# Seven half-size products for the first 512 rows of the last FFN and MLP block

## The chip, the cores and the metric

One core of one Trainium2 chip. The metric is the device time of one execution in microseconds. The kernel before was run three times: 2468.09, 2470.43 and 2472.05 us, median 2470.43 us. A further execution was profiled; its rows are read below.

## What is computed

Two stacks of two layers on 512 tokens of width 1024, all in float32. The parts that the change touches are the four feed-forward units, two of each kind:

```python
def swiglu_ffn(x, w_gate, w_up, w_down):          # first stack, layers 0 and 1, inner width 2816
    return (jax.nn.silu(x @ w_gate) * (x @ w_up)) @ w_down

x = layer_norm(ALPHA * x + y, ln_ffn_g[l], ln_ffn_b[l])

def sq_relu_mlp(h, w_up, w_down):                 # second stack, two layers, inner width 4096
    u = jax.nn.relu(h @ w_up)
    return (u * u) @ w_down
```

After FFN 0 comes a pooling mixer, after FFN 1 the first unit of the second stack, a gated linear attention (GLA). After MLP 0 comes a sliding-window attention, after MLP 1 the output norm.

## The kernel before, in words

The residual `r` stays on chip as four tiles of 128 tokens by 1024. A matrix product in float32 is made as three matmuls (`mm3`, lines 178 to 182) of a high and a low part of each operand: `split` (L151) rounds on ScalarE (L152, the high part) and subtracts on VectorE (L153, the low part). Weights are split the same way, 512 KB raw at a time; where a norm's gain goes into them, the splits are L172 and L173. There are four buffers for split weights, five for raw ones, and eight PSUM banks.

The inner width of a feed-forward unit is worked through in blocks: 1024, 1024 and 768 for an FFN, four times 1024 for an MLP. `hidden` (L941 and L1065) computes a block's activations in chunks of 512 inner rows. The product of a finished block with the down weights is added into `r` by `down_steps` (L235): instead of eight products of quarter blocks it makes seven, of sums and differences of the quarters (a Strassen-Winograd scheme). The sums are VectorE work: of the activations (`sum`), and of the weights (`chain`, from raw weights that come by DMA on SyncE's queue). Each product leaves its two PSUM banks through `resid` (L450), one addition into `r` per bank and place. `weave` (L226) alternates steps of `down_steps` with steps of `hidden` for the next block.

The last block has no next block. Its activations are split once, plainly (`hidh`, `hidl`), and `lin_out` (L361) multiplies them with the down weights in the order of line 376, tile by tile, into one bank per tile and half, followed by the residual addition. When both halves of a tile are there, `ln_tile` (L443; statistics L436 and L438, the two passes L447 and L448, the power of the variance on GpSimd in `rstd`, L423) normalizes it, and the callback of the next unit transposes it on TensorE. For GLA this is `next_unit` (L635): sum of squares on ScalarE (L615), `rstd` on GpSimd, scaling on ScalarE (L640) into `z`, then eight transposes per tile (L415) and their splits into `xTh` and `xTl`. For FFN 0 it is `next_pool` (L589), and key products from the stored memory (`kv_k`, L809, called at L1253) stand between.

The order on each engine is set by the tile framework's scheduler from priorities and its own costs; each engine then runs its list in that order, so that an instruction that waits holds up what stands behind it.

Of the kernel before, what the change touches and what calls it, by code (L numbers as in the profile page):

```python
# [11 lines left out]
F32R = mybir.dt.float32r  # L12
# [60 lines left out]
class Net:  # L73
# [151 lines left out]

    def weave(self, main, side, per):  # L226

        main, side = iter(main), iter(side)
        for _ in main:
            for _ in range(per):  # L230
                next(side, None)
        for _ in side:
            pass

    def down_steps(self, h, W, k0, first, ahead=60):  # L235
# [6 lines left out]
        nc = self.nc  # L242
        lo, hi = slice(0, 256), slice(256, 512)
        a11, a21, a12, a22 = h[0][:, :, lo], h[0][:, :, hi], h[1][:, :, lo], h[1][:, :, hi]
        sums = self.slot([128, 2, 4, 256], name="sum")
        s1, s2 = sums[:, 0], sums[:, 1]
        chain = self.slot([128, 4, 512], name="chain")
        tt = nc.vector.tensor_tensor
        done = set()

        def left(src):
            d = self.slot([128, 2, 4, 256], F32R, "A")
            self.split(d[:, 0], d[:, 1], src)
            return d

        def block(i, j):
            return [self.raw2(W, k0 + 4 * i + k, 512 * j) for k in (0, 2)]

        def plain(i, j):
            return [self.wsplit(b) for b in block(i, j)]  # L260

        def halves(t):
            return [t[:, 0:2], t[:, 2:4]]

        def product(ops, banks, start):
            d, us = ops
            for t in range(2):
                tk = slice(t * 128, t * 128 + 128)
                for k in range(4):
                    u = us[k // 2]  # L270
                    self.mm3(banks[t], d[:, 0, k, tk], d[:, 1, k, tk], u[:, 0, k % 2], u[:, 1, k % 2],
                             start and k == 0, k == 3, skip_group_check=not start)

        def out(i, j, banks, op=ALU.add):
            for t in range(2):
# [660 lines left out]
    def ffn(self, l, nxt, aside):  # L936
        nc, a = self.nc, self.a
        xT = self.pair_view(self.hi, self.lo)
        lg, lb = self.gains("ln_ffn", l)

        def hidden(b0, bw, to, split):  # L941
            for c in range(-(-bw // 512)):
                w = min(512, bw - c * 512)
                sg = self.slot([128, 4, 512], name="sg")
                to.append(sg)
                silu = lambda f, ps, t0, t1, sg=sg: nc.scalar.activation(sg[:, f, t0:t1], ps, AF.Silu)

                def ev_up(f, ps, t0, t1, sg=sg, c=c):
                    s = sg[:, f, t0:t1]
                    nc.vector.tensor_tensor(s, s, ps, ALU.mult)  # L950
                    if split:
                        self.split(split[0][c][:, f, t0:t1], split[1][c][:, f, t0:t1], s)
                if b0 == 0 and c == 0:
                    self.lin_a(xT, a["ffn_wg"][l], 0, silu, halves=True)
                else:
                    yield from self.lin_steps(xT, a["ffn_wg"][l], b0 + c * 512, silu, w)
                yield from self.lin_steps(xT, a["ffn_wu"][l], b0 + c * 512, ev_up, w)

        h = []
        for _ in hidden(0, 1024, h, None):  # L960
            pass
        for b0, bw in ((1024, 1024), (2048, 768)):
            more = []
            out = self.new_xT("hid", 2) if bw < 1024 else None
            self.weave(self.down_steps(h, a["ffn_wd"][l], (b0 - 1024) // 128, b0 == 1024),
                       hidden(b0, bw, more, out), 2)
            h = more
        self.lin_out(self.pair_view(*out), a["ffn_wd"][l], False, (lg, lb), nxt, aside=aside, k0=16, nk=6)

# [88 lines left out]
    def mlp(self, l, nxt):  # L1060
        nc, a = self.nc, self.a
# [2 lines left out]

        def hidden(b, to, split):  # L1065
            for c in range(2):
                if not split:
                    to.append(self.slot([128, 4, 512], name="h"))

                def ev_up(f, ps, t0, t1, c=c):  # L1070
                    u = self.tmp()[:, :t1 - t0]
                    nc.scalar.activation(u, ps, AF.Relu)
                    if split:
                        nc.vector.tensor_tensor(u, u, u, ALU.mult)
                        self.split(split[0][c][:, f, t0:t1], split[1][c][:, f, t0:t1], u)
                    else:
                        nc.vector.tensor_tensor(to[c][:, f, t0:t1], u, u, ALU.mult)
                if b == 0 and c == 0:
                    self.lin_a(xT, W, 0, ev_up, halves=True, gain=g)
                else:  # L1080
                    yield from self.lin_steps(xT, W, b * 1024 + c * 512, ev_up, 512, gain=g)

        h = []
        for _ in hidden(0, h, None):
            pass
        for b in range(1, 4):
            more = []
            out = self.new_xT("hid") if b == 3 else None
            self.weave(self.down_steps(h, a["w_down_2"][l], 8 * b - 8, False), hidden(b, more, out), 1)
            h = more  # L1090
        self.lin_out(self.pair_view(*out), a["w_down_2"][l], False, None, nxt, k0=24, nk=8)

    def rel_bias(self):
        nc, a = self.nc, self.a
# [204 lines left out]
```

## Time and profile before

| what | us |
|---|---|
| median of three runs | 2470.43 |
| profiled execution, device time | 2471.44 |
| its span in the profile | 2469.6 |
| TensorE matmuls busy | 2414.4 (98%) |
| VectorE busy | 1509.4 (61%) |
| ScalarE busy | 1024.4 (41%) |

The page names PE for TensorE, DVE for VectorE, ACT for ScalarE, POOL for GpSimd and SP for SyncE. Busy matmuls overlap in the pipeline, so that a full row says that PE waited for nothing, not that it ran at its peak; the spacing of the starts gives the rate. Some 1.8 us of the device time lie outside the span. The mean granted clock of the execution was 0.989.

### The profile page before, as it was taken

Reading aid. Unit: us, or ns where it says so; the run is one execution under the profiler, and the core shown is the slowest. Engines: PE = TensorE matmul, PEld = TensorE weight load, DVE = VectorE, ACT = ScalarE, POOL = GpSimd, SP = SyncE. Lnnn points to the kernel's source line nnn. Section 1 sums busy time; section 2 is a strip of 40 time slices with the busy share of each in tenths; the row PEclk is TensorE's granted clock in tenths of the full one; section 3 lists DMA queues with packets and bytes.
Section 4 is the critical chain, followed back from the end, with each engine's and each line's share of the span. In section 5 each row is a group of like instructions: output and inputs, shape, how many; then the busy total and the mean of one; then the engine's idle time right before and its main releaser. Section 6 shows DMA issues by size and latency. Waiting matters only on the chain.

```text
span 2469.6 us, 30360 instructions
## 1 busy us (share of the span) xinstructions
PE 2414.4 (98%) x12094; PEld 2010.3 (81%) x12094; DVE 1509.4 (61%) x1994; ACT 1024.4 (41%) x1620; POOL 180.5 (7%) x219
## 2 busy tenths in 40 slices
PE   8989999999999999999999999999999999999998
PEld 8877787888888997888888786888888877888887
DVE  4799475555566766455566423466876467487674
ACT  3653343233333343233334633534444456444443
POOL 1151200000000000000002003200000100000000
PEclk9999899999999999999999999999999999999999
DMA  6333122235344342334434123235553411144452
GB/s 234 103 103 111 54 83 81 84 112 171 109 143 153 126 133 77 94 132 141 141 124 132 60 86 42 87 111 171 179 172 119 161 62 52 60 171 150 155 173 77
DMA packets 148990, 291.92 MB, mean 118 GB/s; under 512 B 9449, under 2 KB 15909, under 8 KB 148592
## 3 DMA queue, kind: packets, MB, share of 16 engines
q1 hardware_dynamic: 146176, 282.17, 34.4%
q0 software_dynamic: 2096, 6.76, 1.4%
q8 instruction: 95, 1.56, 0.2%
q10 hardware_dynamic: 576, 1.05, 0.1%
q14 instruction: 47, 0.39, 0.0%
HBM read 286.77 MB, written 6.32 MB: 119 GB/s over the span
## 4 chain that ended last, share of the span: by engine, by line
PE 88%; DVE 7%; ACT 2%; issue 1%; DMA 1%; POOL 0%; SPq 0%; POOLq 0%; DVEq 0%; ACTq 0%
PE mm L180 23%; PE mm L181 23%; PE mm L182 23%; PE aux L182 5%; PE aux L180 4%; PE aux L181 4%; DVE acc L686 2%; PE aux L415 2%; PE aux L742 1%; DVE w L153 1%; PE mm L769 1%; PE mm L766 1%; PE aux L1219 0%; DVE bn L436 0%; ACT A L152 0%
## 5 line engine op out<-in xcount | busy, mean ns | idle before, releaser
L181 PE MATMUL mm<-xTl,w 128*128 128x512 f32 (+1 forms) x1696 | 614.3, 363 | 2.2 <-DVE xTl L153 2.2
L180 PE MATMUL mm<-xTh,w 128*128 128x512 f32 (+1 forms) x1696 | 611.4, 363 | 2.8 <-ACT w L172 1.8
L182 PE MATMUL mm<-xTh,w 128*128 128x512 f32 (+1 forms) x1696 | 574.0, 362 | 0.0
L153 DVE TENSOR_TENSOR w<-raw,w 128x1024 fp32r<-128x1024 f32 (+1 forms) x286 | 340.4, 1195 | 349.2 <-ACT w L152 348.9
L152 ACT ACTIVATE w<-raw 128x1024 fp32r<-128x1024 f32 (+1 forms) x286 | 293.6, 1030 | 579.4 <-PE mm L182 460.3
L180 PEld LDWEIGHTS mm<-xTh,w 128*128 128x128 f32 x1696 | 320.5, 190 | 53.2 <-ACT w L172 2.6
L181 PEld LDWEIGHTS mm<-xTl,w 128*128 128x128 f32 x1696 | 321.6, 190 | 50.9 <-DVE xTl L153 2.4
L182 PEld LDWEIGHTS mm<-xTh,w 128*128 128x128 f32 x1696 | 320.4, 190 | 48.8
L173 DVE SCALAR_TENSOR_TENSOR w<-raw,gains_T,w 128x512 fp32r<-128x512 f32 (+1 forms) x200 | 140.7, 736 | 122.1 <-ACT w L172 121.6
L172 ACT ACTIVATE w<-raw,gains_T 128x512 fp32r<-128x512 f32 (+1 forms) x200 | 131.1, 707 | 149.0 <-PE mm L182 141.6
L180 PE MATMUL aux<-w,A 128*128 128x512 f32 x440 | 169.6, 391 | 2.1 <-ACT A L152 2.1
L181 PE MATMUL aux<-w,A 128*128 128x512 f32 x440 | 171.4, 390 | 0.0
L182 PE MATMUL aux<-w,A 128*128 128x512 f32 x440 | 170.1, 391 | 1.1 <-DVE A L153 0.7
L181 PE MATMUL mm<-w,xTh 128*128 128x512 f32 (+1 forms) x352 | 135.1, 384 | 0.0
L182 PE MATMUL mm<-w,xTl 128*128 128x512 f32 (+1 forms) x352 | 134.6, 385 | 0.0
L180 PE MATMUL mm<-w,xTh 128*128 128x512 f32 (+1 forms) x352 | 134.6, 385 | 0.0
L152 ACT ACTIVATE w<-chain 128x1024 fp32r<-128x1024 f32 x60 | 63.8, 1063 | 133.4 <-DVE chain L305 52.5
L180 PEld LDWEIGHTS aux<-w,A 128*128 128x128 f32 x440 | 82.6, 188 | 22.7 <-ACT A L152 5.8
L182 PEld LDWEIGHTS aux<-w,A 128*128 128x128 f32 x440 | 82.6, 188 | 21.0 <-DVE A L153 4.1
L181 PEld LDWEIGHTS aux<-w,A 128*128 128x128 f32 x440 | 82.6, 188 | 16.9
L455 DVE TENSOR_TENSOR r<-r,mm 128x512 f32<-128x512 f32 x76 | 51.4, 682 | 55.8 <-PE mm L182 55.8
L153 DVE TENSOR_TENSOR xTl<-aux,xTh 128x512 fp32r<-128x512 f32 x72 | 47.3, 682 | 60.1 <-ACT xTh L152 60.1
(358 smaller groups left out, 4186.9 us busy)
## 6 DMA issues: line engine op xcount, KB each, us to landing
raw<-in_w_down SPq DMA_DIRECT2D x124, 512.0 KB, 3.6
raw<-in_ffn_wd SPq DMA_DIRECT2D x84, 512.0 KB, 3.4
raw<-in_w_up SPq DMA_DIRECT2D x64, 512.0 KB, 4.6
raw<-in_ffn_wg SPq DMA_DIRECT2D x40, 512.0 KB, 3.8
raw<-in_ffn_wu SPq DMA_DIRECT2D x40, 512.0 KB, 3.6
raw<-in_ab_w_in SPq DMA_DIRECT2D x24, 512.0 KB, 4.2
raw<-in_a_w_in SPq DMA_DIRECT2D x24, 512.0 KB, 3.6
raw<-in_xa_wk SPq DMA_DIRECT2D x16, 512.0 KB, 3.4
```

The costliest lines, as they stand in the source:

```text
L152: self.nc.scalar.activation(hi, src, AF.Copy)
L153: self.nc.vector.tensor_tensor(lo, src, hi.bitcast(F32), ALU.subtract)
L172: nc.scalar.activation(u[:, 0, i], raw[:, i], AF.Identity, scale=g)
L173: nc.vector.scalar_tensor_tensor(u[:, 1, i], raw[:, i], g, u[:, 0, i].bitcast(F32), ALU.mult, ALU.subtract)
L180: nc.tensor.matmul(ps, lh, rh, start=start, stop=False, **kw)
L181: nc.tensor.matmul(ps, lh, rl, start=False, stop=False, **kw)
L182: nc.tensor.matmul(ps, ll, rh, start=False, stop=stop, **kw)
L415: self.nc.tensor.transpose(ps[:, j, :], src[:, j * 128:j * 128 + 128], self.ident)
L455: self.nc.vector.tensor_tensor(r, r, ps, op)
L686: nc.vector.scalar_tensor_tensor(dst, src, col, dst, ALU.mult, ALU.add)
L742: nc.tensor.matmul(d[:, h - h0, :], ke[rows, t, h * 128:h * 128 + 128], vh(t, h)[rows, :], start=True, stop=True)
L766: nc.tensor.matmul(o, P[:, h, :], vh(t, h), start=True, stop=False)
```

## The change

`down_steps` takes the number of 128-row pieces of a quarter from the activations that it gets: four as before, or two. In each FFN and MLP, the first 512 inner rows of the last block now also go through it, as quarters of 256 inner rows by 256 tokens; their chunk of `hidden` is no longer split plainly. It runs behind the preceding block's `down_steps` as one list of steps, woven with the last block's `hidden` by a list of counts. `lin_out` keeps 256 inner rows in an FFN (before 768) and 512 in an MLP (before 1024).

```diff
--- before.py
+++ after.py
@@ -225,9 +225,9 @@
 
     def weave(self, main, side, per):
 
-        main, side = iter(main), iter(side)
-        for _ in main:
-            for _ in range(per):
+        side = iter(side)
+        for i, _ in enumerate(main):
+            for _ in range(per[min(i, len(per) - 1)]):
                 next(side, None)
         for _ in side:
             pass
@@ -242,34 +242,35 @@
         nc = self.nc
         lo, hi = slice(0, 256), slice(256, 512)
         a11, a21, a12, a22 = h[0][:, :, lo], h[0][:, :, hi], h[1][:, :, lo], h[1][:, :, hi]
-        sums = self.slot([128, 2, 4, 256], name="sum")
+        nk = h[0].shape[1]
+        sums = self.slot([128, 2, nk, 256], name="sum")
         s1, s2 = sums[:, 0], sums[:, 1]
-        chain = self.slot([128, 4, 512], name="chain")
+        chain = self.slot([128, nk, 512], name="chain")
         tt = nc.vector.tensor_tensor
         done = set()
 
         def left(src):
-            d = self.slot([128, 2, 4, 256], F32R, "A")
+            d = self.slot([128, 2, nk, 256], F32R, "A")
             self.split(d[:, 0], d[:, 1], src)
             return d
 
         def block(i, j):
-            return [self.raw2(W, k0 + 4 * i + k, 512 * j) for k in (0, 2)]
+            return [self.raw2(W, k0 + nk * i + k, 512 * j) for k in range(0, nk, 2)]
 
         def plain(i, j):
             return [self.wsplit(b) for b in block(i, j)]
 
         def halves(t):
-            return [t[:, 0:2], t[:, 2:4]]
+            return [t[:, k:k + 2] for k in range(0, nk, 2)]
 
         def product(ops, banks, start):
             d, us = ops
             for t in range(2):
                 tk = slice(t * 128, t * 128 + 128)
-                for k in range(4):
+                for k in range(nk):
                     u = us[k // 2]
                     self.mm3(banks[t], d[:, 0, k, tk], d[:, 1, k, tk], u[:, 0, k % 2], u[:, 1, k % 2],
-                             start and k == 0, k == 3, skip_group_check=not start)
+                             start and k == 0, k == nk - 1, skip_group_check=not start)
 
         def out(i, j, banks, op=ALU.add):
             for t in range(2):
@@ -941,15 +942,16 @@
         def hidden(b0, bw, to, split):
             for c in range(-(-bw // 512)):
                 w = min(512, bw - c * 512)
+                plain = split if c else None
                 sg = self.slot([128, 4, 512], name="sg")
                 to.append(sg)
                 silu = lambda f, ps, t0, t1, sg=sg: nc.scalar.activation(sg[:, f, t0:t1], ps, AF.Silu)
 
-                def ev_up(f, ps, t0, t1, sg=sg, c=c):
+                def ev_up(f, ps, t0, t1, sg=sg, plain=plain):
                     s = sg[:, f, t0:t1]
                     nc.vector.tensor_tensor(s, s, ps, ALU.mult)
-                    if split:
-                        self.split(split[0][c][:, f, t0:t1], split[1][c][:, f, t0:t1], s)
+                    if plain:
+                        self.split(plain[0][0][:, f, t0:t1], plain[1][0][:, f, t0:t1], s)
                 if b0 == 0 and c == 0:
                     self.lin_a(xT, a["ffn_wg"][l], 0, silu, halves=True)
                 else:
@@ -959,13 +961,17 @@
         h = []
         for _ in hidden(0, 1024, h, None):
             pass
-        for b0, bw in ((1024, 1024), (2048, 768)):
-            more = []
-            out = self.new_xT("hid", 2) if bw < 1024 else None
-            self.weave(self.down_steps(h, a["ffn_wd"][l], (b0 - 1024) // 128, b0 == 1024),
-                       hidden(b0, bw, more, out), 2)
-            h = more
-        self.lin_out(self.pair_view(*out), a["ffn_wd"][l], False, (lg, lb), nxt, aside=aside, k0=16, nk=6)
+        Wd = a["ffn_wd"][l]
+        more = []
+        self.weave(self.down_steps(h, Wd, 0, True), hidden(1024, 1024, more, None), [2])
+        h, last = more, []
+        out = self.new_xT("hid", 1)
+
+        def downs():
+            yield from self.down_steps(h, Wd, 8, False)
+            yield from self.down_steps([last[0][:, 0:2], last[0][:, 2:4]], Wd, 16, False)
+        self.weave(downs(), hidden(2048, 768, last, out), [2, 2, 2, 2, 1])
+        self.lin_out(self.pair_view(*out), Wd, False, (lg, lb), nxt, aside=aside, k0=20, nk=2)
 
 
 
@@ -1064,15 +1070,16 @@
 
         def hidden(b, to, split):
             for c in range(2):
-                if not split:
+                plain = split if c else None
+                if not plain:
                     to.append(self.slot([128, 4, 512], name="h"))
 
-                def ev_up(f, ps, t0, t1, c=c):
+                def ev_up(f, ps, t0, t1, c=c, plain=plain):
                     u = self.tmp()[:, :t1 - t0]
                     nc.scalar.activation(u, ps, AF.Relu)
-                    if split:
+                    if plain:
                         nc.vector.tensor_tensor(u, u, u, ALU.mult)
-                        self.split(split[0][c][:, f, t0:t1], split[1][c][:, f, t0:t1], u)
+                        self.split(plain[0][0][:, f, t0:t1], plain[1][0][:, f, t0:t1], u)
                     else:
                         nc.vector.tensor_tensor(to[c][:, f, t0:t1], u, u, ALU.mult)
                 if b == 0 and c == 0:
@@ -1083,12 +1090,19 @@
         h = []
         for _ in hidden(0, h, None):
             pass
-        for b in range(1, 4):
+        W2 = a["w_down_2"][l]
+        for b in range(1, 3):
             more = []
-            out = self.new_xT("hid") if b == 3 else None
-            self.weave(self.down_steps(h, a["w_down_2"][l], 8 * b - 8, False), hidden(b, more, out), 1)
+            self.weave(self.down_steps(h, W2, 8 * b - 8, False), hidden(b, more, None), [1])
             h = more
-        self.lin_out(self.pair_view(*out), a["w_down_2"][l], False, None, nxt, k0=24, nk=8)
+        more = []
+        out = self.new_xT("hid", 1)
+
+        def downs():
+            yield from self.down_steps(h, W2, 16, False)
+            yield from self.down_steps([more[0][:, 0:2], more[0][:, 2:4]], W2, 24, False)
+        self.weave(downs(), hidden(3, more, out), [1, 1, 1, 1, 0, 1])
+        self.lin_out(self.pair_view(*out), W2, False, None, nxt, k0=28, nk=4)
 
     def rel_bias(self):
         nc, a = self.nc, self.a
```

Where instructions stand, on TensorE at the end of FFN 1 (`mm` with `hidh` is the closing product, one bank per tile and half; `aux` with `z` are the transposes of a tile; the last `mm` rows are GLA's projections). Before:

```order
L180 MATMUL mm_10150<-wb_9936,hidh_9208 128x512 [waits DVE_49]
L181 MATMUL mm_10150<-wb_9941,hidh_9208 128x512
L415 MATMUL aux_10045<-consts,z_10039 128x128 [waits Activation_49]
L415 MATMUL aux_10052<-consts,z_10039 128x128 x4
L182 MATMUL mm_10150<-wb_9941,hidl_9210 128x512
L182 MATMUL mm_10150<-wb_9946,hidl_9211 128x512
L180 MATMUL mm_10201<-wb_9936,hidh_9208 128x512 [waits DVE_49]
L182 MATMUL mm_10201<-wb_9946,hidl_9211 128x512
L415 MATMUL aux_10096<-consts,z_10090 128x128 [waits Activation_49]
L415 MATMUL aux_10103<-consts,z_10090 128x128 [waits DVE_49]
L180 MATMUL mm_10281<-xTh_9964,wz_9954 128x256 [waits Activation_49,Pool_49]
L180 MATMUL mm_10307<-w_10255,xTh_9964 128x512
```

With the change, the same place:

```order
L180 MATMUL mm_10262<-w_10133,hidh_9256 128x512 [waits DVE_49]
L180 MATMUL mm_10270<-wb_10138,hidh_9256 128x512 [waits DVE_49]
L182 MATMUL mm_10270<-wb_10138,hidl_9257 128x512
L180 MATMUL mm_10309<-wb_10138,hidh_9256 128x512 [waits DVE_49]
L182 MATMUL mm_10309<-wb_10138,hidl_9257 128x512
L416 MATMUL aux_10201<-consts,z_10195 128x128 [waits Activation_49]
L416 MATMUL aux_10208<-consts,z_10195 128x128 x4
L416 MATMUL aux_10240<-consts,z_10234 128x128 [waits Activation_49]
L416 MATMUL aux_10247<-consts,z_10234 128x128 [waits DVE_49]
L180 MATMUL mm_10377<-xTh_10156,wz_10146 128x256 [waits Activation_49,Pool_49]
L180 MATMUL mm_10403<-w_10351,xTh_10156 128x512
```

Before, the transposes of tile 0 stand 28 matmuls ahead of the closing product's last row and those of tile 1 directly behind it; with the change the transposes of both tiles stand behind its last row, one after the other, and the projections behind both.

On VectorE at the same place (`bn` and `mv` are the statistics of a tile, `r_86` is tile 0). Before:

```order
L455 TENSOR_TENSOR r_86<-r_86,mm_10008 128x512 [waits PE_49]
L436 BN_STATS bn_10028<-r_86 128x6 [waits DVE_49]
L438 BN_AGGR mv_10031<-bn_10028 128x2 [waits DVE_49]
L447 SCALAR_TENSOR_TENSOR r_86<-r_86,mv_10031,w4k_7803 128x1024 [waits DVE_49]
L448 SCALAR_TENSOR_TENSOR r_86<-r_86,rs_10033,w4k_7805 128x1024 [waits DVE_49,Pool_49]
L455 TENSOR_TENSOR r_88<-r_88,mm_10059 128x512 [waits PE_49]
L436 BN_STATS bn_10079<-r_88 128x6 [waits DVE_49]
```

With the change:

```order
L456 TENSOR_TENSOR r_86<-r_86,mm_10160 128x512 [waits PE_49]
L456 TENSOR_TENSOR r_88<-r_88,mm_10168 128x512 [waits PE_49]
L456 TENSOR_TENSOR r_110<-r_110,aux_9864 128x512 [waits PE_49]
L437 BN_STATS bn_10184<-r_86 128x6 [waits DVE_49]
...
L456 TENSOR_TENSOR r_112<-r_112,mm_10309 128x512 [waits PE_49]
L437 BN_STATS bn_10317<-r_112 128x6 [waits DVE_49]
L439 BN_AGGR mv_10187<-bn_10184 128x2 [waits DVE_49]
L437 BN_STATS bn_10278<-r_110 128x6 [waits DVE_49]
L437 BN_STATS bn_10317<-r_112 128x6 [waits DVE_49]
L448 SCALAR_TENSOR_TENSOR r_86<-r_86,mv_10187,w4k_7851 128x1024 [waits DVE_49]
L449 SCALAR_TENSOR_TENSOR r_86<-r_86,rs_10189,w4k_7853 128x1024 [waits DVE_49,Pool_49]
```

Before, tile 0 is normalized as soon as its second half is added; now the additions and statistics of all four tiles, ten additions and eight statistics in all, stand ahead of its two passes.

On TensorE at the end of FFN 0, with the change (`mh` is the stored memory, `bands` the pooling of tile 0):

```order
L180 MATMUL mm_6118<-wb_5951,hidh_5069 128x512 [waits DVE_49]
L182 MATMUL mm_6118<-wb_5951,hidl_5070 128x512
L180 MATMUL mm_6179<-mh_5956,w_6161 128x256 [waits DVE_49,Activation_49]
L180 MATMUL mm_6303<-mh_5956,w_6285 128x256 [waits DVE_49,Activation_49]
L603 MATMUL aux_6000<-bands_5964,r_86 128x16 [waits DMASW1_49,DVE_49]
```

The key products stand between the closing product and the first instruction that needs a normalized tile, as they did before.

On VectorE in the woven last block of FFN 1, with the change (`A` are split activations, `w` from `chain` split weight differences):

```order
L153 TENSOR_TENSOR A_9932<-sum_9862,A_9932 128x512 [waits Activation_49]
L153 TENSOR_TENSOR A_9979<-sum_9862,A_9979 128x512 [waits Activation_49]
L456 TENSOR_TENSOR r_88<-r_88,mm_9916 128x512 [waits PE_49]
L153 TENSOR_TENSOR w_9940<-chain_9863,w_9940 128x1024 [waits Activation_49]
L153 TENSOR_TENSOR w_9945<-raw_9943,w_9945 128x512 [waits DMAHW1_49,Activation_49]
L315 TENSOR_TENSOR raw_10023<-raw_10023,raw_10025 128x1024 [waits DMAHW5_49,DMAHW4_49]
L306 TENSOR_TENSOR chain_9863<-raw_9982,chain_9863 128x1024 [waits DMAHW2_49,DVE_49]
L456 TENSOR_TENSOR r_110<-r_110,aux_9962 128x512 [waits PE_49]
L456 TENSOR_TENSOR r_112<-r_112,mm_9963 128x512 [waits PE_49]
L153 TENSOR_TENSOR w_9985<-chain_9863,w_9985 128x1024 [waits Activation_49]
L153 TENSOR_TENSOR w_9990<-raw_9988,w_9990 128x512 [waits DMAHW3_49,Activation_49]
```

None of these stood there before; each product of the added seven needs an `A`, two `w` and a resid of the banks before it.

## Rows read from the trace of the kernel before

**Rows 1.** Section 1 of the page: busy us, share of span, instructions.

```profile
PE 2414.4 (98%) x12094; PEld 2010.3 (81%) x12094; DVE 1509.4 (61%) x1994; ACT 1024.4 (41%) x1620; POOL 180.5 (7%) x219
```

**Rows 2.** Section 4 of the page: the chain of waits, by engine.

```profile
PE 88%; DVE 7%; ACT 2%; issue 1%; DMA 1%; POOL 0%; SPq 0%; POOLq 0%; DVEq 0%; ACTq 0%
```

**Rows 3.** PE's waits, 990:1316, then 740:870 (total us, times, longest).

```profile
PE aux L415 <- DVE r L448: 0.3, 1, 0.3
...
PE aux L415 <- DVE r L448: 0.8, 1, 0.8
```

**Rows 4.** Stretches ending FFN 1: us; PE, PEld, DVE, ACT, POOL busy; clock.

```profile
1260.00:1290.00 30.00, 30.00 (x134) 24.80 (x133) 19.84 (x24) 11.47 (x14) 0.00 (x0) 1.00 0.29 87
1290.00:1317.00 27.00, 27.00 (x121) 22.36 (x120) 12.40 (x16) 9.54 (x13) 3.47 (x4) 1.00 0.44 145
1317.00:1340.00 23.00, 23.00 (x103) 19.02 (x103) 18.18 (x26) 8.92 (x14) 6.15 (x10) 1.00 0.43 139
1340.00:1357.00 17.00, 16.66 (x83) 13.81 (x82) 16.01 (x24) 8.85 (x14) 5.05 (x8) 1.00 0.31 98
```

**Rows 5.** DVE by line, whole span: busy us, mean ns, idle before.

```profile
L455 DVE TENSOR_TENSOR r<-r,aux 128x512 f32<-128x512 f32 x96 | 65.3, 680 | 23.5 <-PE aux L182 23.4
L153 DVE TENSOR_TENSOR w<-chain,w 128x1024 fp32r<-128x1024 f32 x60 | 71.9, 1217 | 11.1 <-ACT w L152 11.1
```

**Rows 6.** What DVE waited for, 1180 to 1316 us.

```profile
DVE raw L314 <- DMA raw<-in_ffn_wd: 7.1, 2, 4.8
DVE chain L326 <- DMA raw<-in_ffn_wd: 3.0, 2, 2.7
```

**Rows 7.** PE timeline, closing product of FFN 1 (start, us, line, operation).

```profile
1316.16 0.39 PE L180 MATMUL mm<-w,hidh 128*128 128x512 f32 x1
...
1342.46 1.03 PE L415 MATMUL aux<-consts,z 128*128 128x128 f32 x8
...
1349.70 1.03 PE L415 MATMUL aux<-consts,z 128*128 128x128 f32 x8
1351.07 0.36 PE L180 MATMUL mm<-xTh,wz 128*128 128x256 f32 x1 [0.34 <-ACT xTh L152]
```

**Rows 8.** DVE timeline, the same place.

```profile
1327.69 1.28 DVE L455 TENSOR_TENSOR r<-r,mm 128x512 f32<-128x512 f32 x2 [2.35 <-PE mm L182]
1328.89 1.28 DVE L436 BATCH_NORM_STATS2 bn<-r 128x6 f32<-128x512 f32 x2
...
1331.77 1.28 DVE L447 SCALAR_TENSOR_TENSOR r<-r,mv,w4k 128x1024 f32<-128x1024 f32 x1
1333.83 1.28 DVE L448 SCALAR_TENSOR_TENSOR r<-r,rs,w4k 128x1024 f32<-128x1024 f32 x1 [0.78 <-POOL rs L430]
...
1340.58 2.06 DVE L173 SCALAR_TENSOR_TENSOR w<-raw,gains_T,w 128x512 fp32r<-128x512 f32 x3
```

**Rows 9.** ACT timeline, the same place.

```profile
1335.15 1.06 ACT L615 ACTIVATE z<-r 128x1024 f32<-128x1024 f32 x1 [13.14 <-DVE r L448]
...
1337.24 1.15 ACT L640 ACTIVATE z<-r,rs 128x1024 f32<-128x1024 f32 x1 [0.94 <-POOL rs L430]
...
1343.09 1.09 ACT L152 ACTIVATE xTh<-aux 128x512 fp32r<-128x512 f32 x2 [0.91 <-PE aux L415]
...
1346.15 1.15 ACT L640 ACTIVATE z<-r,rs 128x1024 f32<-128x1024 f32 x1 [0.94 <-POOL rs L430]
```

**Rows 10.** Stretch after FFN 0, columns as in rows 4.

```profile
807.00:830.00 23.00, 23.00 (x195) 22.78 (x194) 14.41 (x17) 8.18 (x13) 1.80 (x2) 1.00 0.33 110
```

**Rows 11.** Stretches around an idle PE, columns as in rows 4.

```profile
1398.00:1400.00 2.00, 0.00 (x0) 0.00 (x0) 1.01 (x2) 1.97 (x4) 0.00 (x0) 1.00 0.02 6
1400.00:1402.00 2.00, 1.87 (x7) 1.67 (x8) 0.88 (x2) 2.00 (x5) 0.00 (x0) 0.55 0.82 258
1402.00:1404.00 2.00, 2.00 (x7) 1.57 (x6) 2.00 (x5) 2.00 (x5) 0.00 (x0) 0.59 0.01 4
1404.00:1406.00 2.00, 2.00 (x10) 1.60 (x10) 1.80 (x3) 0.77 (x2) 0.00 (x0) 1.00 0.42 101
```

## The prediction

> **What bounds the kernel now.** I read the page first. TensorE is busy for 98% of the span [rows 1] and the chain of waits lies on it for 88% [rows 2]: the reader is to see that an edit pays here only if it shortens TensorE's list, and that any wait put on TensorE counts in full. VectorE's 61% [rows 1] is an average, so I read the waits of TensorE next, around the ends of both FFNs: 0.3 us in 326 us that end with FFN 1's hidden part, and 0.8 us at the end of FFN 0 [rows 3]. Then the stretches [rows 4]: up to 1340 us TensorE never pauses, while VectorE is busy for 32.2 us of the 57 us from 1260 to 1317, then for 18.2 of 23 and 16.0 of 17 us. So VectorE, loose through most of the unit, is already close to full where the closing product, the residual additions and the layernorm meet. That is where the change works.
>
> **What it saves.** 512 inner rows done plainly are 4 token tiles x 2 halves x 4 pieces x 3 matmuls = 96; as seven products they are 7 x 2 x 2 x 3 = 84. Twelve fewer in each of four units: 48. In the closing product of FFN 1, 116 matmuls take from 1316.16 to 1342.46 us [rows 7], 0.2267 us each. So the saving is 2.7 us per unit, **10.9 us** in all, if TensorE does not wait.
>
> **What it adds.** On VectorE, per unit: 14 more residual additions (0.68 each [rows 5], 9.5 us), three more splits of weight differences and four more differences (1.22 each, the first in [rows 5], 8.5 us), four sums of activations and seven splits of activations at half the size (11 x 0.68, 7.5 us), less four plain splits (2.7 us): some 23 us a unit. On SyncE's queue five more loads of 512 KB a unit, because the differences read quarters of the weights again.
>
> *The woven part.* The 23 us fall into the last 54 to 57 us of hidden work, on top of the 32.2 us there: about 55 us of VectorE beside about as much of TensorE. They fit only without gaps. The waits for loads of the weight differences were 0.3 to 4.8 us each before [rows 6], and TensorE hid them; the added part has four such groups, in a line with no slack: the order of VectorE shows an activation split, a residual addition and two weight splits in turn. The bounds are 0 (everything is issued early enough) and 5 us a unit (one such load in full). I take **2 us** for each FFN, whose last hidden chunk of 256 is short cover, and **1 us** for each MLP, whose 512 give nearly twice as much.
>
> *The end of FFN 1.* I call the start of the closing product T. Before, it held 144 matmuls; tile 0 was normalized while tiles 2 and 3 were still multiplied, and the first projection came at 1351.07, T + 34.9 us [rows 7], of which TensorE was idle for 0.34 us. Now it holds 48 matmuls, and 12 of the last half-size product are mixed in: TensorE is through at T + 13.6. VectorE can start on the first result at about T + 5 (22 matmuls). From there to tile 0's last pass the new order has ten additions (0.60 apart [rows 8], 6.0 us), eight statistics (0.64 each [rows 8], 5.1 us), four gain splits (0.69 each [rows 8], 2.7 us), the aggregate (0.2 us), and the two passes, each 1.28 us [rows 8]: 16.6 us. Tile 0 is normalized at about T + 21.6. Then ScalarE squares, GpSimd takes the root, ScalarE scales: 1335.15 to 1338.39, 3.3 us [rows 9]. The transposes of tile 0 start at T + 25 and TensorE has been idle for 11 us. Tile 1 stands ahead of the projections too: ScalarE first splits tile 0's transposes and then runs the same chain for tile 1. It did so before in the same order: transposes begun at 1342.46, split by 1344.18, tile 1 scaled by 1347.30 [rows 7, 9], 4.8 us after the beginning, of which TensorE's transposes take 1: 4 us more idle. With the 1.4 us from these transposes to the first projection [rows 7] the projections begin at T + 31. They came at T + 34.9 before, but with 84 matmuls (19.0 us) more between. That is **15 us of new idle time** (34.9 - 19.0 = 15.9, against 31). The bounds: 11 if tile 1's chain overlaps tile 0's fully, 19 if the closing product's first result finds VectorE still 4 us behind with the woven part.
>
> *The clock.* After two us without a matmul, from 1398 to 1400, the granted clock was 0.55 and 0.59 for the next 4 us, the lower of its two levels (1.2 GHz), and full again after 1404 [rows 11]. Four us at that level are some 2 us of work lost. Here TensorE falls idle twice, with only 8 transposes between; I take the price once, **2 us**, behind the second gap, since the transposes after the first are short. The bounds are 0 and 4 (once behind each). The Trainium skill, "TensorE: Matmul & The Clock Gate", Part 1, says that the array's clock is halved by default and released by activity that lasts; the fall to 0.55 agrees. By that rule 8 transposes would not release it, the slow time would lie behind both gaps, and the sum would be 2 us higher.
>
> *The end of FFN 0.* The same 60 matmuls are followed by key products of the stored memory, 195 matmuls in 23.0 us by the row after FFN 0 [rows 10], ahead of the first instruction that needs a normalized tile (the order puts it 110 matmuls behind the closing product, and the other 82 among the pooling's own). TensorE has work to about T + 26; tile 0 is ready at about T + 25 with the extra weight splits in VectorE's list. Cost 0; if the cover fell short it would be 1 to 3 us.
>
> *The ends of the MLPs.* `lin_out` keeps 96 matmuls, 21.8 us, and there is no layernorm: tile 0 is complete after 36 of them, 8 us, and scaled 4 us later [rows 9], long before TensorE is through. Cost 0. After MLP 1 the last tile's path to the output is unchanged.
>
> **The sum.** FFN 0: -2.7 + 2 = -0.7. FFN 1: -2.7 + 2 + 15 + 2 = +16.3. MLPs: 2 x (-2.7 + 1) = -3.4. In all +12 us on the profiled execution's 2471.4 us, which lies 1.0 us above the median of the runs: **2482 us** on the scale of the median, +0.5%.
>
> **Rivals.**
> (a) *Faster: the end of FFN 1 costs little.* If the ten additions and the statistics do not stand between TensorE's last row and tile 0 (VectorE far enough ahead, or GLA's weights and projections filling the gap), only the saving and the woven waits are left: -10.9 + 6 = -5, or 2465 us; with no woven waits 2460. It turns on one number, TensorE's idle time between the closing product and GLA's first projection: below some 5 us the change is faster. For it: before, VectorE was at 16.0 of 17 us there and TensorE still did not wait [rows 4]. Against it: TensorE's list is in order and has nothing else between; 0.15.
> (b) *No difference: half of it.* Idle time of 7 to 10 us at FFN 1 and no slow clock gives -10.9 + 6 + 8 = +3: 2473 us; 0.17.
> (c) *Slower still: VectorE binds in all four woven last blocks.* 55 us of its work in 55 us of time; then each load wait of up to 4.8 us [rows 6] lands on TensorE: -10.9 + 4 x 5 + 15 + 2 = +26, 2496 us. For it: 8.5 of VectorE's 23 added us a unit hang on loads, which come by the same queue as the hidden part's weights. Against it: TensorE waited for 0.3 us in the woven blocks before [rows 3]; 0.1.
> (d) *The change does not do what it says.* The order shows the 84 product rows per unit and the shorter `lin_out`; 0.
>
> **How the numbers follow.** A measurement of this kernel can tell about 0.2%, 5 us. The forecast's own case (idle time of 11 to 19 us, woven waits of 2 to 12 us in all, clock 0 to 4 us) reaches from -10.9 + 2 + 11 = +2 to -10.9 + 12 + 19 + 4 = +24, most of it from +6 to +17; chance 0.58. The range takes in (b) and part of (a), and of (c) the lower half: 2464 to 2492 us. Slower by over 0.2%: most of the forecast and (c), 0.64. Within 0.2%: (b) and the forecast's lower end, 0.19. Faster: (a) and little more, 0.17.
>
> **What would show it.** Right: in the changed profile PE has a wait of about 10 us for ACT's `z` at the first transposes after FFN 1's closing product, one of about 4 us at the next, and a clock near 0.55 behind; at the end of FFN 0 and in the MLPs no wait over 1 us; PE's busy time falls by about 11 us, DVE's rises by about 90. Wrong: if those two waits are together below 5 us, the forecast falls to (a); if waits of 2 us or more stand at the `A` and `w` of the added products in all four units, it rises to (c).

## The result and the profile after

The changed kernel took 2486.2 us (median of four runs, 2481.0 to 2488.1) beside 2470.9 us of the kernel before: ratio 1.006, 95% interval 1.0048 to 1.0073, so 12 to 18 us more. Forecast were 2482 us, and a wait of TensorE at the end of FFN 1 as the cause. The profiled execution took 2484.4 us with a span of 2482.7.

The busy times and the chain of waits, from the page of the changed kernel:

```profile
PE 2404.2 (97%) x12046; PEld 1996.0 (80%) x12046; DVE 1588.5 (64%) x2106; ACT 1040.7 (42%) x1644; POOL 178.2 (7%) x219
...
PE 85%; DVE 9%; ACT 3%; issue 2%; DMA 1%; POOL 1%; SPq 0%; POOLq 0%; DVEq 0%; ACTq 0%
```

Against [rows 1], TensorE has 48 matmuls fewer and is busy for 10.2 us less, VectorE for 79 us more; the chain of waits lies on TensorE for 85% instead of 88% [rows 2]. What TensorE waited for, in FFN 0 and its end, in FFN 1 up to the closing product, and from there into GLA (total, times, longest; the changed kernel's line numbers are one higher at L416 to L456, and some more further down):

```profile
PE aux L180 <- ACT w L152: 1.5, 2, 0.8
PE mm L181 <- DVE w L153: 1.1, 2, 0.6
PE aux L181 <- DVE w L153: 0.4, 1, 0.4
...
PE mm L180 <- ACT hidh L152: 2.2, 1, 2.2
PE aux L180 <- ACT w L152: 1.5, 2, 0.9
PE aux L181 <- DVE w L153: 0.4, 1, 0.4
...
PE aux L416 <- ACT z L641: 16.8, 2, 11.9
PE mm L180 <- POOL rs L428: 0.4, 1, 0.4
```

The second part answers to [rows 3], where TensorE waited for 0.3 us: the woven part, with the wait for `hidh` at the closing product's start, now has 4.1 us of waits besides. The third part is the forecast's two gaps, 11.9 and 4.9 us. TensorE's timeline there, from the closing product's first matmul to GLA's first projection, answers to [rows 7]:

```profile
1331.16 0.50 PE L180 MATMUL mm<-w,hidh 128*128 128x512 f32 x1 [2.18 <-ACT hidh L152]
...
1357.62 1.97 PE L416 MATMUL aux<-consts,z 128*128 128x128 f32 x8 [11.89 <-ACT z L641]
...
1364.49 1.97 PE L416 MATMUL aux<-consts,z 128*128 128x128 f32 x8 [4.91 <-ACT z L641]
1366.90 0.55 PE L180 MATMUL mm<-xTh,wz 128*128 128x256 f32 x1 [0.44 <-POOL rs L428]
```

VectorE at the same place (with one row of the woven part), and the stretches with their clock (columns as in [rows 4]):

```profile
1326.09 0.29 DVE L992 TENSOR_TENSOR raw<-raw,gains_T 128x128 f32<-128x128 f32 x1 [4.19 <-DMA raw<-in_a_w_in]
...
1337.94 1.29 DVE L456 TENSOR_TENSOR r<-r,mm 128x512 f32<-128x512 f32 x2
...
1352.78 1.28 DVE L449 SCALAR_TENSOR_TENSOR r<-r,rs,w4k 128x1024 f32<-128x1024 f32 x1
```

```profile
1346.00:1350.00 4.00, 0.00 (x0) 0.00 (x0) 4.00 (x7) 0.00 (x0) 0.00 (x0) 1.00 0.43 114
1350.00:1356.00 6.00, 0.00 (x0) 0.00 (x0) 5.36 (x8) 1.15 (x2) 1.38 (x5) 0.50 0.21 79
1356.00:1362.00 6.00, 1.97 (x8) 1.57 (x8) 3.69 (x5) 3.38 (x5) 1.55 (x3) 0.50 0.00 0
...
1368.00:1370.00 2.00, 2.00 (x6) 1.52 (x6) 1.27 (x2) 1.29 (x2) 0.31 (x1) 0.50 0.20 52
1370.00:1372.00 2.00, 2.00 (x10) 1.62 (x9) 0.00 (x0) 1.05 (x3) 0.74 (x2) 0.87 0.00 0
```

VectorE works through additions, statistics and gain splits without a pause and ends tile 0's last pass at 1354.06, 22.9 us after the closing product's first matmul. TensorE stands still from 1345.7 to 1357.6, its clock falls to 0.50 by 1350 and comes back behind 1370; the transposes take 1.97 us instead of 1.03.

**By stages.** Lengths in the profiled executions, in us. FFN 0: from its first `sg` activation to that of FFN 1. FFN 1: from there to the first transposes of `qt` in GLA. The next two end with the last matmul of each MLP's closing product. The rows below the change are the experiments.

| kernel | FFN 0 | FFN 1 | GLA, MLP 0 | attention, MLP 1 |
|---|---|---|---|---|
| before | 550.0 | 390.2 | 537.6 | 524.2 |
| the change | 549.2 | 411.6 | 538.2 | 521.6 |
| e1, all but FFN 1 | 549.2 | 390.7 | 534.6 | 528.1 |
| e2, FFN 1 only | 550.2 | 410.8 | 541.2 | 532.9 |
| e3, MLPs only | 550.0 | 390.2 | 534.6 | 521.7 |
| e5, L992 on GpSimd | 549.4 | 407.4 | 536.7 | 526.2 |
| e6, extra matmuls | 549.6 | 408.7 | 538.4 | 526.8 |
| e9, other order | 550.0 | 408.1 | 534.5 | 531.3 |

Where the code is the same, FFN 0 repeats within 0.9 us in this table, and FFN 1 within 1.6 (411.6 here, 410.8 in e2, 410.0 in e10 below), so their columns tell effects of 2 us. The last two can't: the third scatters by 3.9 us in equal code, the last by 11 us in code that differs by 2.7, for a reason told at the end. The time ahead of FFN 0, in no column and the same code in every kernel, ran from 453.4 to 459.9 us.

Medians are read against the kernel before of the same set of runs: it took 2470.9 us beside the change and 2468.0 to 2468.1 beside e1 to e9.

### The profile page after: what moved, and what is told of

It is laid out like the page before. It is cut to its first block, busy times and chain, and to the rows that moved or that the text cites. A ratio compares the mean times of both kernels' runs of the same rounds, so it can differ in the third digit from the quotient of the medians.

```text
span 2482.7 us, 30467 instructions
## 1 busy us (share of the span) xinstructions
PE 2404.2 (97%) x12046; PEld 1996.0 (80%) x12046; DVE 1588.5 (64%) x2106; ACT 1040.7 (42%) x1644; POOL 178.2 (7%) x219
## 4 chain that ended last, share of the span: by engine, by line
PE 85%; DVE 9%; ACT 3%; issue 2%; DMA 1%; POOL 1%; SPq 0%; POOLq 0%; DVEq 0%; ACTq 0%
PE mm L180 22%; PE mm L181 21%; PE mm L182 21%; PE aux L182 5%; PE aux L180 5%; PE aux L181 5%; DVE acc L687 2%; PE aux L416 2%; DVE w L153 1%; PE aux L743 1%; PE mm L770 1%; PE mm L767 1%; DVE A L153 1%; DVE bn L437 1%; DVE r L456 1%
## 5 line engine op out<-in xcount | busy, mean ns | idle before, releaser
L153 DVE TENSOR_TENSOR w<-raw,w 128x1024 fp32r<-128x1024 f32 (+1 forms) x294 | 349.0, 1196 | 295.0 <-ACT w L152 294.6
L152 ACT ACTIVATE w<-raw 128x1024 fp32r<-128x1024 f32 (+1 forms) x294 | 301.2, 1031 | 557.1 <-PE mm L182 416.4
L180 PE MATMUL aux<-w,A 128*128 128x512 f32 x528 | 204.4, 393 | 4.9 <-ACT w L152 3.0
L182 PE MATMUL aux<-w,A 128*128 128x512 f32 x528 | 204.5, 392 | 2.5 <-DVE A L153 2.1
L181 PE MATMUL aux<-w,A 128*128 128x512 f32 x528 | 206.1, 390 | 0.8 <-DVE w L153 0.8
L152 ACT ACTIVATE w<-chain 128x1024 fp32r<-128x1024 f32 x72 | 76.4, 1063 | 169.9 <-DVE chain L306 67.5
L180 PEld LDWEIGHTS aux<-w,A 128*128 128x128 f32 x528 | 99.0, 188 | 31.2 <-ACT A L152 6.7
L182 PEld LDWEIGHTS aux<-w,A 128*128 128x128 f32 x528 | 99.1, 188 | 27.1 <-DVE A L153 6.8
L456 DVE TENSOR_TENSOR r<-r,aux 128x512 f32<-128x512 f32 x140 | 95.0, 683 | 36.5 <-PE aux L182 36.2
L181 PEld LDWEIGHTS aux<-w,A 128*128 128x128 f32 x528 | 99.2, 188 | 21.6 <-DVE w L153 1.6
L153 DVE TENSOR_TENSOR w<-chain,w 128x1024 fp32r<-128x1024 f32 x72 | 86.8, 1222 | 22.4 <-ACT w L152 22.4
```

The costliest lines, as they stand in the source:

```text
L152: self.nc.scalar.activation(hi, src, AF.Copy)
L153: self.nc.vector.tensor_tensor(lo, src, hi.bitcast(F32), ALU.subtract)
L180: nc.tensor.matmul(ps, lh, rh, start=start, stop=False, **kw)
L181: nc.tensor.matmul(ps, lh, rl, start=False, stop=False, **kw)
L182: nc.tensor.matmul(ps, ll, rh, start=False, stop=stop, **kw)
L456: self.nc.vector.tensor_tensor(r, r, ps, op)
```

## The experiments

**Where the loss is.** Three kernels take the change in some units only. e1 calls the old function for FFN 1:

```diff
-net.ffn(1, net.next_unit, net.gla_prepare)
+net.ffn_old(1, net.next_unit, net.gla_prepare)
```

> The change in FFN 0 and both MLPs; FFN 1 as before, with its last 768 inner rows the plain way. Theory A, the loss sits at the end of FFN 1 alone (waits of 11.9 and 4.9 us at the transposes there, and the lower clock around them): 36 matmuls fewer give -8.2 us, woven waits in FFN 0 take back about 2: 6 us faster than the kernel before, about 2465. Theory B, the added VectorE work and weight loads cost TensorE in each of the four units alike: three quarters of the +15 us, about 2482.

e2 calls the old functions for FFN 0 and both MLPs:

```diff
-net.ffn(0, net.next_pool, net.mem_again)
+net.ffn_old(0, net.next_pool, net.mem_again)
-net.mlp(0, net.next_unit)
+net.mlp_old(0, net.next_unit)
...
```

> The change in FFN 1 alone. Theory A: -2.7 us of matmuls, +16.8 of new waits at the transposes, +2 to 4 for the clock, +3 in the woven part: 19 to 21 us slower than the kernel before, about 2490, slower than the whole change. Theory B: a quarter of the loss, +4 us, about 2475.

e3 calls the old function for both FFNs.

> The change in both MLPs alone. Theory A: 24 matmuls fewer, -5.4 us, with at most 1 us of waits: 2465 to 2467 us. Theory B: half of the loss, +7 us, about 2478.

e1 took 2465.9 us, ratio 0.999 (0.9978 to 1.0002), not told apart from the kernel before; e2 2493.8, ratio 1.011 (1.0088 to 1.0131); e3 2463.9, ratio 0.9978 (0.9964 to 0.9993), each beside 2468.0 us of the kernel before. Theory B falls: the loss is all in FFN 1, and e2 is slower than the whole change. (For e1 theory A expected 6 us less than the kernel before; the medians show 2.1, at most 5.4 by the interval; FFN 0 and the lengths of the MLPs further down add up to 5.8.) TensorE's waits around FFN 1's end, in e1 and then in e2:

```profile
PE mm L180 <- ACT xTh L152: 0.3, 1, 0.3
PE aux L182 <- DVE A L153: 0.3, 1, 0.3
```

```profile
PE aux L416 <- ACT z L641: 16.8, 2, 11.9
```

e2's median is 26 us above the kernel before, more than the 19 to 21 expected; its stage FFN 1 has 20.6 of it. Where the other 5 lie was not settled: the profiled execution is the longest of e2's six (2503.3 us), and in it the last two columns are 12.3 us above the kernel before, in equal code.

**What the closing product has to cover.** e7 leaves FFN 1's layernorm out of the change, e8 out of the kernel before.

```diff
-self.lin_out(self.pair_view(*out), Wd, False, (lg, lb), nxt, ...)
+self.lin_out(self.pair_view(*out), Wd, False, None if l == 1 else (lg, lb), nxt, ...)
```

> The whole change, without FFN 1's layernorm (statistics and both passes left out; the rest is kept, so the output differs). Theory A, the layernorm of four tiles queued on VectorE behind ten additions is what the short closing product can't cover: the first wait at the transposes falls from 11.9 to below 2 us, the second to 2 to 4 us, and from the closing product's first matmul to GLA's first projection it takes about 20 us instead of 35.7. Rival, TensorE's order (transposes behind the closing product) and ScalarE's chain cost it without the layernorm too: the first wait stays above 6 us.

> The kernel before, without FFN 1's layernorm, for comparison with the previous run. Both theories: TensorE did not wait there, so the time stays within 2 us of the kernel before, 34.9 us from the closing product to the first projection. By theory A the change is then worth about -3 to 0 us between these two kernels instead of +13 to +15; by the rival still +8 or more.

TensorE's timeline in e7:

```profile
1333.93 0.50 PE L180 MATMUL mm<-w,hidh 128*128 128x512 f32 x1 [1.99 <-ACT hidh L152]
...
1349.43 1.06 PE L416 MATMUL aux<-consts,z 128*128 128x128 f32 x8
...
1354.35 1.09 PE L416 MATMUL aux<-consts,z 128*128 128x128 f32 x8 [3.86 <-ACT z L641]
...
1356.43 1.12 PE L416 MATMUL aux<-consts,z 128*128 128x128 f32 x4 [0.99 <-ACT z L641]
1357.19 0.56 PE L180 MATMUL mm<-xTh,wz 128*128 128x256 f32 x1
```

The same two ends in e8:

```profile
1313.42 0.39 PE L180 MATMUL mm<-w,hidh 128*128 128x512 f32 x1
...
1348.34 0.36 PE L180 MATMUL mm<-xTh,wz 128*128 128x256 f32 x1
```

From the closing product to the first projection it took 23.3 us (35.7 with the layernorm) and in e8 34.9, as before. The first gap is gone; the second is 3.9 us, and tile 2's transposes, which now stand ahead of the projections too, waited 1.0. The stage FFN 1 takes 399.2 us in e7 and 387.3 in e8. So the first gap is the layernorm on VectorE, as theory A has it; the second is the chain from tile 0's transposes to tile 1's scaling on ScalarE, with its root on GpSimd, and it stays without the layernorm. The expectation for the totals missed: 2485.8 us beside 2471.4, one execution each, still 14 us, the size that it gave to the rival. This stage holds 11.9 of them, where with the layernorm it holds 21.5. So the layernorm makes 9.6 us of the loss. The rest is there without it: the stage is 4.8 us longer up to the closing product than the 72 matmuls moved there take (waits of 2.0, 1.5 and 0.4 us), 7.4 longer from there to the first projection than 84 matmuls less would leave it (34.9 - 19.0 = 15.9), and 2.4 longer behind, less the 2.7 saved.

**Why FFN 0 loses nothing.** e10 takes the key products behind FFN 0's closing product away from the change, e11 from the kernel before.

```diff
-net.kv_k(1, net.mT)
+net.K = net.slot([128, 8, 256], name="K")
+net.nc.gpsimd.memset(net.K, 0.0)
```

> The whole change, with layer 1's key products (192 matmuls behind FFN 0's closing product, 23 us of cover) left out and zeros in their place, so the output differs. Theory A, the short closing product costs nothing at FFN 0 only because these products cover the layernorm: without them TensorE waits at the pooling of tile 0 for VectorE's last pass, 5 to 9 us, and 1 to 4 us more at the next tiles; from the closing product's first matmul to the pooling's first product about 15 us more than the 60 matmuls and the pooling take. Rival, FFN 1's loss is made by its own next unit (squares, root, scaling and transposes), not by the layernorm: at FFN 0, where none of these follow, the waits stay below 2 us in all.

> The kernel before without the same key products. Theory A: its closing product of 144 matmuls covers the layernorm of the first tiles, so that TensorE waits for at most 2 us in all before the pooling's first product; the difference between these two kernels' FFN 0 ends is then 5 to 10 us more than between the change and the kernel before. Rival: no wait in either, no difference.

TensorE's wait for a normalized tile, in e10 and then in e11:

```profile
PE aux L603 <- DVE r L449: 6.2, 1, 6.2
```

```profile
PE aux L605 <- DVE r L448: 1.1, 1, 1.1
```

Without the cover the stage FFN 0 takes 546.3 us with the change and 529.7 without it: 16.6 us lost, where with the cover 0.8 were won. The rival falls, since no next unit like FFN 1's follows here. The wait itself (6.2 us against 1.1) is the smaller part, and no wait followed at the next tiles. The pooling's short matmuls behind it ran on at the lower clock, as the stretches of e10 show, beside one of e11's pooling:

```profile
800.00:810.00 10.00, 6.80 (x32) 6.80 (x33) 9.66 (x13) 0.60 (x1) 6.07 (x7) 0.50 0.00 0
810.00:820.00 10.00, 10.00 (x48) 10.00 (x48) 6.69 (x11) 4.14 (x7) 0.84 (x1) 0.50 0.51 159
820.00:830.00 10.00, 10.00 (x49) 10.00 (x48) 3.65 (x6) 1.79 (x3) 0.00 (x0) 0.50 0.60 210
```

```profile
810.00:820.00 10.00, 10.00 (x86) 10.00 (x86) 10.00 (x18) 2.50 (x5) 0.79 (x2) 1.00 0.67 220
```

The expectation, 5 to 10 us between the two differences, left the clock out: 16.6 lost against 0.8 won makes 17.4. How near the cover is to its end, the change's own rows show, VectorE's last pass of tile 0 and TensorE's first pooling product:

```profile
803.60 1.28 DVE L449 SCALAR_TENSOR_TENSOR r<-r,rs,w4k 128x1024 f32<-128x1024 f32 x1
...
806.46 0.29 PE L603 MATMUL aux<-bands,r 128*128 128x16 f32 x2
```

The tile was ready at 804.88, 1.6 us before it was needed.

**The parts of FFN 1.** e5 moves one multiplication off VectorE.

```diff
-nc.vector.tensor_tensor(raw, raw, g0, ALU.mult)
+nc.gpsimd.tensor_tensor(raw, raw, g0, ALU.mult)
```

> The whole change, with the gain multiplication of GLA's gate weights (L992) on GpSimd instead of VectorE. In the changed kernel it waited 4.2 us for a load on GpSimd's queue, with the last weight difference's split, two additions and the products for the last hidden chunk behind it. Theory C, this one wait makes the 2.2 us that TensorE waits for hidh at the start of FFN 1's closing product: that wait falls to below 0.5 us, the waits of 11.9 and 4.9 us behind stay, and the kernel is 1.5 to 2.5 us faster than the change. Rival: the weight loads themselves are late (VectorE waited 8.3 us for them), so hidh still waits 1 to 2 us and the time stays within 1 us.

TensorE's waits in e5, up to the closing product and behind it:

```profile
PE aux L180 <- ACT w L152: 1.5, 2, 0.9
PE aux L181 <- DVE w L153: 0.4, 1, 0.4
...
PE aux L416 <- ACT z L641: 16.3, 2, 11.4
```

The wait for `hidh`, 2.2 us in the change and 0.9 to 2.0 in e2, e6, e7 and e10, is gone and the rest stands. Theory C holds for the wait: the largest of the woven part's came from a load of GLA's on another queue. As a gain in time it is not shown: the stage FFN 1 is 407.4 us against 410.0 to 411.6, but the median of 2484.2 us is 16.1 above its kernel before (1.0064, 1.0046 to 1.0081), where the change's was 15.3 above.

e6 keeps TensorE at work in the gaps.

```diff
 self.lin_out(self.pair_view(*out), Wd, False, (lg, lb), nxt, aside=aside, k0=20, nk=2)
+if l == 1:
+    ps = self.bank([128, 512])
+    for i in range(44):
+        nc.tensor.matmul(ps, out[0][0][:, 0, :128], out[0][0][:, 0, :], start=True, stop=True)
+    for i in range(14):
+        nc.tensor.matmul(ps, self.hi[0][:, 0, :128], out[0][0][:, 0, :], start=True, stop=True)
```

> The whole change, with 58 more matmuls whose result nobody reads: 44 on TensorE between FFN 1's closing product and tile 0's transposes (10 us of the 11.9 idle), 14 between the transposes of tiles 0 and 1 (3.2 us of 4.9). They cover nothing and should lengthen nothing; they keep TensorE at work. Theory D, the idle stretches also cost the lower clock, once for the transposes and once for the first projections: granted clock 1.00 there, transposes back from 1.97 to about 1.03 us each, first projections 0.23 apart; 3 to 4 us faster than the change, 2482. Rival, the clock costs only behind the second gap as forecast: 1.5 to 2 us. Rival, no gain: the same 2486, the clock falls all the same.

TensorE's timeline in e6, and its stretches:

```profile
1344.78 10.13 PE L978 MATMUL mm<-hidh 128*128 128x512 f32 x44
1356.87 1.09 PE L416 MATMUL aux<-consts,z 128*128 128x128 f32 x8 [1.95 <-ACT z L641]
1358.21 5.06 PE L980 MATMUL mm<-hidh,xTh 128*128 128x512 f32 x14 [0.25 <-ACT xTh L152]
1363.11 1.03 PE L416 MATMUL aux<-consts,z 128*128 128x128 f32 x8
1365.44 0.35 PE L180 MATMUL mm<-xTh,wz 128*128 128x256 f32 x1 [1.29 <-POOL rs L428]
```

```profile
1350.00:1354.00 4.00, 4.00 (x19) 3.34 (x18) 3.86 (x6) 0.66 (x1) 0.56 (x1) 1.00 0.17 67
1358.00:1360.00 2.00, 1.79 (x5) 1.47 (x6) 1.77 (x4) 1.68 (x4) 0.23 (x1) 0.65 0.00 0
1360.00:1362.00 2.00, 2.00 (x6) 1.54 (x6) 0.91 (x1) 0.17 (x1) 1.92 (x4) 0.50 0.00 0
1362.00:1364.00 2.00, 2.00 (x14) 1.59 (x12) 1.62 (x3) 1.32 (x2) 0.31 (x1) 1.00 0.00 0
```

The clock held where the first gap had been, and the transposes were back at 1.03 to 1.09 us; but behind the 1.95 us that were left idle it fell once more, and the 14 matmuls took 5.06 us instead of 3.2. The stage FFN 1 is 2.9 us shorter, 0.5 of it in a shorter wait for `hidh`. From the closing product to `qt` it took 81.3 us, where the change, e2 and e10 took 83.7, 83.7 and 83.3: the clock costs 2.0 to 2.4 us, between the two readings. The median doesn't show it: 2487.8 us is 19.7 above its kernel before, with 5.2 us more than the change in the last column. As a gain in time it failed.

e9 puts tile 0's passes further ahead on VectorE, and 12 matmuls between the transposes of tiles 0 and 1; it contains e5.

```diff
-    yield from self.down_steps([last[0][:, 0:2], last[0][:, 2:4]], Wd, 16, False)
+    held.append(self.down_steps([last[0][:, 0:2], last[0][:, 2:4]], Wd, 16, False, swap=l == 1))
+    if l == 1:
+        for _ in range(5):
+            yield next(held[0])
+    else:
+        yield from held.pop()
...
+            if mid and (half, t) == (0, 2):
+                for _ in mid:
+                    pass
             if half == 0:
```

> The whole change, with L992 on GpSimd, and in FFN 1 the seven products in another order (the third of the tail, whose result goes to tokens 0 to 255, ahead of the two that go to tokens 256 to 511 alone), the last of them issued in the program behind the closing product of tiles 0 and 1. On VectorE tile 0's two passes then stand behind six additions and five statistics instead of ten and eight, and 12 matmuls stand on TensorE between the transposes of tiles 0 and 1. Theory A, FFN 1's end is set by what stands ahead of tile 0's passes on VectorE and by what covers it on TensorE: from the closing product's first matmul to GLA's first projection about 26 us instead of 35.7, the first wait 7 to 9 us instead of 11.9, the second about 1.5 instead of 4.9; with L992 the kernel is 10 to 12 us faster than the change, 2474 to 2476, and still slower than the kernel before by 4 to 8. Rival, the chain from a tile's last addition to its transposes sets it whatever stands ahead: the first wait stays above 10 us and the gain is below 4 us.

TensorE's timeline in e9:

```profile
1351.06 1.11 PE L429 MATMUL aux<-consts,z 128*128 128x128 f32 x4 [8.31 <-ACT z L654]
1353.59 1.11 PE L429 MATMUL aux<-consts,z 128*128 128x128 f32 x4 [1.41 <-DVE xTl L153]
1356.94 0.79 PE L180 MATMUL aux<-w,A 128*128 128x512 f32 x1 [2.24 <-ACT A L152]
...
1362.23 1.46 PE L429 MATMUL aux<-consts,z 128*128 128x128 f32 x8
1364.42 0.36 PE L180 MATMUL mm<-xTh,wz 128*128 128x256 f32 x1 [0.74 <-ACT xTh L152]
```

The first gap is 8.3 us, as theory A gave it. But the 12 matmuls waited 2.2 us for their own split, ran at the lower clock (0.43 us apart), and the transposes waited for a bank: 33.3 us instead of 26 to the first projection, and 408.1 for the stage, no shorter than e5's 407.4. The median, 2490.5 us, is 22.4 above its kernel before, where 10 to 12 less than the change was expected; the last column has 9.7 us more. What stands ahead of tile 0 on VectorE sets the first gap; taking it away alone gained nothing.

## Why the prediction held, point by point

- *The saving.* 48 matmuls fewer, as worked out; busy time 10.2 us less for 10.9. VectorE has 79 us more for the forecast's 90.
- *FFN 0.* Forecast -0.7, measured -0.8 by stages, which is within their scatter. Up to the closing product the stage grew by 18.2 us; the 72 matmuls moved there are 16.3, so 1.9 for the forecast's 2. Its end cost nothing: with T as the start of its own closing product, tile 0 was ready at T + 25.2 and needed at T + 26.8, where T + 25 and T + 26 were worked out. That the key products are the reason is shown by e10 and e11. The fallback price of 1 to 3 us was far off: 16.6 without the cover.
- *The end of FFN 1.* The mechanism was right and its size too small: 15 us of idle time forecast, with 2 for the clock; 19.8 measured (35.7 us from the closing product to the first projection, where 34.9 - 19.0 = 15.9 would be as before). Against the forecast's T + 31: the first result came 1.8 us later (T + 6.8), the queue behind took about as long as summed, tile 0 was ready 1.3 us later (22.9 for 21.6) and its transposes 1.5; the second gap was 0.9 longer; the transposes took twice 0.94 more; and 0.4 went to a wait for `rs`. Of the loss e7 gives 9.6 us to the layernorm; the chain of tile 1 and the clock stay without it. From the projections to `qt` 1.1 us came back (47.9 for 49.1).
- *The clock.* Priced at 2 us, once behind the second gap. The rows have 0.50 from 1350 to 1370, through both gaps and what lies between, so the place was wrong; e6 puts the price at 2.0 to 2.4, so the size was right. The rule that the prediction took from the Trainium skill, "TensorE: Matmul & The Clock Gate", Part 1, by which both gaps are paid, had the better place; the trace agrees with it there (0.50 before, at and behind the first transposes), not with the 4 us that the prediction made of it.
- *The woven part.* 2 us were forecast for each FFN. FFN 0 had 1.9. FFN 1's stage up to the closing product grew by 21.8 us, 72 matmuls moved there are 16.3: 5.4, not 2, and above the upper bound of 5 (in e10, with the same code, 4.2). 2.2 of that is L992, which the working didn't see: it counted weight loads on SyncE's queue and left out that a GLA load on GpSimd's queue, waited for on VectorE, stands between the weight differences (VectorE waited 1.8 us for it in the kernel before, too, where it cost TensorE nothing). That is the term that was mis-sized most for its price.
- *The MLPs.* Forecast -1.7 each. By the median of e3, -4.2 for both. From an MLP's first ReLU activation to its last closing matmul, MLP 0 took 328.6 us in the four kernels with the old function (before, e2, e8, e11) and 325.6 or 325.7 in the eight with the new one, MLP 1 326.8 and 324.7 or 324.8: -2.9 and -2.0. So of the 1 us of waits forecast for each, none was lost in MLP 0 and 0.7 in MLP 1.
- *The sum.* -2.7 + 5.4 + 19.8 - 1.1 = +21.4 for FFN 1 (stage: 21.5), -0.8 for FFN 0 and -5.0 for the MLPs by their lengths give +15.6; the medians have +15.3. The forecast of +12 lacks 5 us in FFN 1 and has 1.5 us too much in the MLPs. That +12 came near +15.3 is in part luck: these two misses cancel in part, and in the profiled executions the four columns are 18.6 us apart and the time ahead of FFN 0, in equal code, -5.9.
- *The rivals.* (a) and (b) needed idle time below 10 us at FFN 1; it was 16.8. (c) needed waits of 2 us or more in all four units; the longest in the MLPs was 0.9.

The version that is faster than both kernels is e3, with the change in the MLPs alone: 0.9978, interval 0.9964 to 0.9993.

## What to carry to other kernels

A product with fewer matmuls pays only where something else covers the work that hung behind the longer one: before shortening the last product of a unit, add up what VectorE must do between its first result and the first instruction that needs a finished tile, and look for what TensorE has to do meanwhile. Here the same edit won under 1 us at FFN 0, where independent products follow, and lost 21 us at FFN 1, where none do. Where an order is in line, look also for loads of the next unit that stand in it: one wait of 4.2 us on VectorE stood behind one of 2.2 on TensorE.

## What the runs showed of the hardware that was not expected

The sliding-window attention is the same code in all of these kernels; from MLP 0's closing product to MLP 1's first activation it took 196.9 to 207.6 us in the twelve profiled executions. The same 20 us of it, 80 to 100 us behind MLP 0's closing product, first in the changed kernel and then in e9:

```profile
2033.00:2053.00 20.00, 18.99 (x99) 14.42 (x99) 17.20 (x40) 16.01 (x51) 1.49 (x2) 1.00 0.17 54
```

```profile
2029.00:2049.00 20.00, 17.47 (x59) 13.43 (x59) 11.86 (x29) 12.73 (x40) 0.90 (x2) 0.50 0.01 1
```

99 matmuls at full clock in one, 59 at 0.50 in the other. Both have the same wait of 1.98 us for `ol` some 77 us behind the closing product; behind it the clock fell in e9 and held in the changed kernel. So it was with GLA's wait for `qt`: 2.25 us in the kernel before, with 0.55 behind it [rows 11], and 2.38 us in e8, with 1.00 behind it (1394 to 1400). It differs between executions of one program as well: the twelve of e1 took 2460.8 to 2470.7 us, the shortest at a mean granted clock of 0.994, the longest at 0.988. So medians of a few executions can lie some us off for this alone, even where they repeat closely (e9: 2489.7 to 2491.6), and the stages had to carry the reading. What decides it was not tried. How long the lower clock lasted was not expected either: 30 us behind one wait of 6.2 in e10, with TensorE busy for all of the last 20 of them, and 20 us around the two gaps of the change.
